# DeltaNet gate sums taken earlier, query sums and the second group's inverses later, six extra products at the last FFN

## The chip, the core and the metric

The kernel runs on one core of one Trainium2 chip, in one launch. The core has five engines that run side by side and each take their instructions strictly in the order in which the program gives them: TensorE (PE in the profile: matrix products and transposes into PSUM; PEld is its loading of weights), VectorE (DVE), ScalarE (ACT), GpSimd (POOL) and SyncE (SP, which here issues most DMAs). Semaphores tie them together: an instruction that waits holds up everything behind it on its own engine.

The metric is the device time of one execution in microseconds, lower is better. Before the change it is 1917.68 us, the median of three executions (1916.97 to 1921.42).

## What is computed

Two layers work on 256 context tokens and 256 latent tokens with 1024 channels. Each layer is a half-step SwiGLU FFN, a token mixer, and another half-step FFN; each of the three is preceded by an RMS norm with shift and scale, and added to the stream through a gate. The mixer of the first layer is a bidirectional gated DeltaNet in chunks of 64 tokens, that of the second is windowed attention. The output is the latent stream.

```python
def _swiglu(h, w1, w2):
    a, b = jnp.split(h @ w1, 2, axis=-1)
    return (jax.nn.silu(a) * b) @ w2

# DeltaNet, per head and chunk
gc = jnp.cumsum(_to_chunks(g, DN_CHUNK), axis=-1)
decay = jnp.exp(jnp.where(causal, gc[..., :, None] - gc[..., None, :], -jnp.inf))
kb = k * beta[..., None]
lower = jnp.where(strict, jnp.einsum('nhcid,nhcjd->nhcij', kb, k) * decay, 0.0)
uw = lax.linalg.triangular_solve(lower, rhs, left_side=True, lower=True, unit_diagonal=True)
qk = jnp.einsum('nhcid,nhcjd->nhcij', q, k) * decay
```

`g` and `beta` come from 32 columns of the input projection (the gates); `gc` are their running sums. `q` and `k` are projected, pass a short convolution over time and a SiLU, and are divided by their lengths, for which the sums of squares are needed. `triangular_solve` is the inverse of a 64 x 64 triangle for each chunk, head and direction.

## The kernel before

All activations lie with the channels on the 128 partitions and the 512 tokens (context, then latent) along the free dimension: 8 tiles of 128 x 512. The large products run in fp32r with each factor split in a high and a low part, three products in place of one (`mm3`). The weights stream in through SP's queue; ACT makes each high part, DVE or POOL the low one (`_split`).

**A planner writes the order.** The program is put out by Python generators ("tasks") under a small planner, `Sched`. It keeps a clock that each product advances by an assumed duration: in `mm`, 107 ns for an fp32r product of 256 columns and 213 for one of 512. It also keeps assumed times at which each tile will be ready. A task yields the time for which it wants to be left alone: `self.at(tile)` until the tile is expected, `self.spare(tile)` 2,500 ns longer. When the clock reaches a task's due time, its next step is put out, between two products of the main stream. The planner settles only the order on each engine's queue; on the chip the semaphores decide the time. While the main program waits in `Sched.until`, it puts out no products of its own, and the clock jumps from one due time to the next.

**The DeltaNet stage** (`deltanet`) projects 33 units through `units` and `halves_first`: the gates, then K, Z (an output gate), Q and V of heads 0 to 3, then K, V, Q and Z of heads 4 to 7. The first four units (gates, K heads 0 to 2) are done half by half, all context tokens first, 24 products of 256 columns for a unit's half. Each unit has a task `dn_unit`: ACT scales the product (the middle tap of the convolution), DVE adds four taps, ACT takes the SiLU; for K and V, PE transposes the result; for Q, ACT squares it; for Z, DVE applies a gain and the result is stored to DRAM (`ZD`).

Beside these run:
- `dn_gates`: softplus and sigmoid of the gates on ACT and DVE, the per-token values `gs` and `lb`; then five small fp32 products that sum `gs` over the chunk; then, out of the sums, `glb` and `kdl` on DVE, `eg` and `aS` on ACT, `neg` on DVE.
- `dn_kq(g)` for a group of four heads: `dn_ss` sums the squares of Q (four products with a matrix of ones), copies them to SBUF on ACT, transposes them and takes their logarithm (`lnq`, used by `dn_out` at the stage's end); then the key-query products (`dn_pairs`), multiplied on DVE with the decays. For group 1 it then stores Q and K to DRAM (`QD`, `KTD`).
- `dn_group(g)`: `dn_prep` (decay matrices), `dn_solve` (the inverses), then the four heads' recurrences `dn_chain` with `dn_expand`, which spreads the inverses and key-query blocks. For group 1 it waits for `kq_done[1]` and for group 0's chains, and then loads V, K, Q and the decayed K (`VD`, `KTD`, `QD`, `KD`) back from DRAM.
- `dn_solve` inverts 32 x 32 diagonal blocks in 31 steps on DVE, and then forms the off-diagonal blocks on PE, for each of two chunk pairs `qp`: 32 small products, a copy `w` on ACT, 32 products with `w`, and a write-back into `UB`.

**The last FFN** (`last_ffn`) works on latent tokens alone. Its norm ends in two products with a matrix of ones (`rstd`). The task `last_tokens` then transposes the eight activation tiles (16 transposes into four PSUM tiles), for the output is written with tokens on the partitions. Behind it `last_pairs` starts the FFN's first products as soon as the normed input `H` is there, tile by tile. `self.OH` are the attention's outputs, which lie in SBUF since the layer's middle.

Of the kernel before, what the change touches and what calls it, by code (L numbers as in the profile page):

```python
# [213 lines left out]
class Kernel:  # L214
# [706 lines left out]
    def last_tokens(self):  # L921

        nc = self.nc
        self.XT, self.gate = [], []

        while not self.rs_there:
            yield 100
        pss = []
        for tb in range(2):
            for fh in range(2):  # L930
                ps = self.mmt()
                for c in range(4):
                    self.tr(ps[:, 128 * c:128 * c + 128], self.X[4 * fh + c][:, 256 + 128 * tb:384 + 128 * tb])
                pss.append(ps)
        yield 8000
        for ps in pss:
            x = self.u()
            self.act(out=x, in_=ps, func=AF.Copy)
            self.XT.append(x)
            yield 1000  # L940
        pss = ps = None
        while (1, 8) not in self.ready:
            yield 1000
        gd = self.dp.tile([1024], F32, name="gd", tag="gd")
        nc.sync.dma_start(out=gd.rearrange("(k p) -> p k", p=128), in_=self.mod[1, 8][:, 1, :])
        for fh in range(2):
            g = self.u()
            nc.sync.dma_start(out=g, in_=gd[512 * fh:512 * fh + 512].partition_broadcast(128))
            self.gate.append(g)
            g = None  # L950
        yield 1000
# [250 lines left out]
    def dn_gates(self, ps):  # L1202

        nc = self.nc
        sb = self.u()
        for o, i in zip(self.pieces(sb, True), self.pieces(ps, False)):
            self.act(out=o[0:64], in_=i[0:64], func=AF.Copy)
        yield self.at(sb)
        p2 = self.cht()
        for q in range(4):  # L1210
            self.tr(p2[:, 64 * q:64 * q + 64], sb[0:64, 128 * q:128 * q + 128], 64)
        yield self.at(p2)
        t, y = self.u(), self.u()
        nc.vector.tensor_reduce(out=y[:, 0:128].rearrange("p (q c) -> p q c", q=4), axis=AX.X, op=ALU.add,
                                in_=p2[:, 0:256].rearrange("p (q j c) -> p q c j", q=4, j=2))
        x = t[:, 0:128].rearrange("p (q d k h) -> p q d k h", q=4, d=2, k=2)
        pv = y[:, 0:128].rearrange("p (q d k h) -> p q d k h", q=4, d=2, k=2)
        dtb = self.dtb.rearrange("p (d h) -> p d h", d=2).unsqueeze(1).broadcast_to([128, 4, 2, 8])
        nc.vector.tensor_tensor(out=x[:, :, :, 0, :], in0=pv[:, :, :, 0, :], in1=dtb, op=ALU.add)
        nc.vector.tensor_scalar(out=x[:, :, :, 1, :], in0=pv[:, :, :, 1, :], scalar1=-1.0, scalar2=None, op0=ALU.mult)  # L1220
        self.act(out=t[:, 128:256], in_=t[:, 0:128], func=AF.Abs)
        self.act(out=t[:, 256:384], in_=t[:, 128:256], func=AF.Exp, scale=-1.0)
        self.act(out=t[:, 384:512], in_=t[:, 256:384], func=AF.Ln, bias=1.0)
        nc.vector.scalar_tensor_tensor(out=t[:, 128:256], in0=t[:, 0:128], scalar=0.0, in1=t[:, 384:512],
                                       op0=ALU.max, op1=ALU.add)
        sp = t[:, 128:256].rearrange("p (q d k h) -> p q d k h", q=4, d=2, k=2)
        self.gs = self.const([128, 2, 4, 8], "gs")
        lb = self.const([128, 2, 4, 8], "lb")
        for e in range(2):
            for half in range(2):  # L1230
                d = e ^ half
                rw = slice(64 * half, 64 * half + 64)
                ea = self.ea[rw, 8 * d:8 * d + 8].unsqueeze(1).broadcast_to([64, 4, 8])
                nc.vector.scalar_tensor_tensor(out=self.gs[rw, e], in0=sp[rw, :, d, 0, :], scalar=-1.0, in1=ea,
                                               op0=ALU.mult, op1=ALU.mult)
                nc.vector.tensor_scalar(out=lb[rw, e], in0=sp[rw, :, d, 1, :], scalar1=-1.0, scalar2=None, op0=ALU.mult)
        yield self.spare(self.gs)
        p3 = self.cht()
        gf = self.gs.rearrange("p e q h -> p (e q h)")
        for e in range(2):  # L1240
            self.mm(p3[:, 32 * e:32 * e + 32], self.tri[e], gf[:, 32 * e:32 * e + 32])
        self.mm(p3[:, 64:128], self.bones, gf)
        for i in range(2):
            self.mm(p3[:, 128 + 64 * i:192 + 64 * i], self.hsel[i], gf)
        self.glb = self.const([128, 2, 4, 8], "glb")
        fl = lambda t: t.rearrange("p e q h -> p (e q h)")
        nc.vector.tensor_tensor(out=fl(self.glb), in0=p3[:, 0:64], in1=fl(lb), op=ALU.subtract)
        self.kdl = self.const([128, 2, 4, 8], "kdl")
        nc.vector.tensor_tensor(out=fl(self.kdl), in0=p3[:, 64:128], in1=fl(self.glb), op=ALU.subtract)
        self.eg = self.const([128, 2, 4, 8], "eg")  # L1250
        self.act(out=fl(self.eg), in_=p3[:, 0:64], func=AF.Exp)
        self.aS = self.const([128, 2, 2, 4, 8], "aS")
        self.act(out=self.aS.rearrange("p i e q h -> p (i e q h)"), in_=p3[:, 128:256], func=AF.Exp)
        self.neg = self.const([128, 2, 4, 8], "neg")
        nc.vector.tensor_scalar(out=self.neg, in0=self.eg, scalar1=-1.0, scalar2=None, op0=ALU.mult)
        self.kdw = self.const([128, 2, 4, 8], "kdw")
        self.mj = self.const([128, 2, 4, 8], "mj")
        self.lnk = self.const([128, 4, 8], "lnk")
        self.irho = self.const([128, 4, 8], "irho")
        self.lnq = self.const([128, 4, 8], "lnq")  # L1260
# [60 lines left out]
    def dn_ss(self, sq, g, dst):  # L1321

        ps = self.mmt()
        for i in range(4):
            self.mm(ps[32 * i:32 * i + 32, :], self.ones1, sq[4 * g + i], tp=(0, 32 * i), ns=230)
        sb = self.u()
        self.act(out=sb, in_=ps, func=AF.Copy)
        yield self.at(sb)
        ps = self.mmt()
        for q in range(4):  # L1330
            self.tr(ps[:, 128 * q:128 * q + 128], sb[:, 128 * q:128 * q + 128])
        self.act(out=dst[:, :, 4 * g:4 * g + 4], in_=ps.rearrange("p (q i r) -> p q i r", q=4, i=4)[:, :, :, 0],
                 func=AF.Ln, bias=self.eps)
        for i in range(4):
            del sq[4 * g + i]
# [93 lines left out]
    def dn_solve(self, g):  # L1429
# [53 lines left out]
        for qp in range(2):  # L1483
            combos = []
            for e in range(2):
                for half in range(2):
                    d = e ^ half
                    combos.append((d, 16 * e + 8 * qp, 64 * half + 32 * d, 64 * half + 32 * (1 - d), 32 * (1 - d)))
            ps = self.mmt()
            for i in range(8):  # L1490
                for d, x, ra, rb, cb in combos:
                    self.mm(ps[rb:rb + 32, 32 * i:32 * i + 32], UB[ra:ra + 32, x + i, cb:cb + 32],
                            v3(xt[d])[ra:ra + 32, x + i, :], tp=(ra, rb), ns=27)
            w = self.u()
            self.act(out=w[:, 0:256], in_=ps[:, 0:256], func=AF.Copy)
            wv = w[:, 0:256].rearrange("p (a i) -> p a i", i=32)
            yield self.at(w)
            ps = self.mmt()
            for i in range(8):
                for d, x, ra, rb, cb in combos:  # L1500
                    self.mm(ps[ra:ra + 32, 32 * i:32 * i + 32], wv[rb:rb + 32, i, :], UB[rb:rb + 32, x + i, cb:cb + 32],
                            tp=(rb, ra), ns=27)
            for n, (d, x, ra, rb, cb) in enumerate(combos):
                o, i = UB[ra:ra + 32, x:x + 8, cb:cb + 32], ps[ra:ra + 32, 0:256].rearrange("p (a i) -> p a i", i=32)
                if n % 2:
                    nc.vector.tensor_scalar(out=o, in0=i, scalar1=-1.0, scalar2=None, op0=ALU.mult)
                else:
                    self.act(out=o, in_=i, func=AF.Copy, scale=-1.0)
# [542 lines left out]
```

## Time and profile before

| | us |
|---|---|
| median of three executions | 1917.68 (1916.97 to 1921.42) |
| the profiled execution | 1922.17 |
| its span, first to last instruction | 1920.4 |
| DeltaNet stage, from the gates' products to the last chain | about 412 to 785 |
| attention stage | about 1595 to 1700 |
| last FFN | about 1721 to 1920 |

All later durations are read from the one profiled execution, in microseconds from the start of its span. In the timeline a row has its start, its duration (of several instructions together, where xN stands), engine, line, operation, what it writes and reads, and in brackets how long the engine had stood idle and what ended that. In rows of stretches stand from:to, length, then the busy time (and number of instructions) of PE, PEld, DVE, ACT and POOL, PE's granted clock, and the share of the DMA engines with GB/s. Nearly all instructions carry the line of a helper (L284 product, L289 transpose, L184 everything recorded for DVE, ACT, POOL and SP), so they are told apart by their tiles and shapes.

### The profile page before, as it was taken

The page shows a single profiled execution, that of the slowest core. Times are in us where ns is not written, and L with a number is a line of the kernel's source. Part 1 is how long each engine was busy: PE and PEld are TensorE (multiplying, and loading weights), DVE is VectorE, ACT ScalarE, POOL GpSimd, SP SyncE. Part 2 cuts the span into 40 slices and gives each one's busy share as a digit, 9 for nine tenths or more (in the row PEclk, how much of TensorE's full clock was granted, in tenths as well). Part 3 has the DMA queues.
Part 4 walks back from the last instruction along what each step waited for, and adds up shares of the span by engine and source line. Part 5 has one row for each costly group of instructions (what it writes and reads, how often), then busy time and mean ns, then how long its engine had stood idle before and what let it go on. Part 6 is the DMA issues. An engine that isn't in the chain of part 4 may idle for free.

```text
span 1920.4 us, 28976 instructions
## 1 busy us (share of the span) xinstructions
PE 1861.0 (97%) x10719; PEld 1525.2 (79%) x10719; DVE 1286.5 (67%) x2124; ACT 966.7 (50%) x2106; POOL 642.2 (33%) x594
## 2 busy tenths in 40 slices
PE   7999999998999999999999999999999999899998
PEld 5878888897777666798888888888888898688887
DVE  4887877755987965578787885745433345967565
ACT  4544534456466545465444444533332348867553
POOL 3343433353546535354343342321200047330000
PEclk9999999999999998999999999999999999999999
DMA  9655554413322252344555454455323325126561
GB/s 294 217 190 188 172 175 154 129 48 123 94 58 76 67 182 83 127 159 160 192 187 191 159 178 162 138 170 190 129 88 110 110 67 122 55 67 191 193 198 66
DMA packets 238708, 271.70 MB, mean 141 GB/s; under 512 B 12343, under 2 KB 189135, under 8 KB 238567
## 3 DMA queue, kind: packets, MB, share of 16 engines
q1 hardware_dynamic: 237703, 269.15, 43.4%
q8 instruction: 84, 1.38, 0.3%
q10 hardware_dynamic: 720, 0.59, 0.1%
q14 instruction: 57, 0.47, 0.1%
q0 software_dynamic: 144, 0.11, 0.0%
HBM read 259.32 MB, written 10.49 MB: 140 GB/s over the span
## 4 chain that ended last, share of the span: by engine, by line
PE 59%; DVE 9%; ACT 3%; issue 2%; POOL 1%; DMA 0%; DVEq 0%; POOLq 0%; ACTq 0%
PE mm L284 58%; DVE u L184 7%; ACT u L184 3%; DVE big L184 1%; PE mm L289 1%; POOL u L184 1%; DVE st L184 0%; DMA u<-XD 0%; ACT ub L184 0%; DVE ub L184 0%; ACT L184 0%; DVEq L184 0%; ACT sc L184 0%; POOLq L184 0%; ACTq L184 0%
## 5 line engine op out<-in xcount | busy, mean ns | idle before, releaser
L284 PE MATMUL mm<-u 128*128 128x512 f32 (+4 forms) x9480 | 1775.5, 353 | 21.5 <-POOL u L184 9.2
L284 PEld LDWEIGHTS mm<-u 128*128 128x128 f32 (+1 forms) x9480 | 1455.9, 185 | 325.1 <-issue 42.0
L184 POOL TENSOR_TENSOR u<-u 128x512 f32<-128x512 f32 (+4 forms) x386 | 425.6, 1108 | 903.9 <-ACT u L184 863.0
L184 ACT ACTIVATE u<-u 128x256 f32<-128x256 f32 (+8 forms) x361 | 170.9, 485 | 448.7 <-DVE u L184 435.4
L184 ACT ACTIVATE u<-mm 128x128 f32<-128x128 f32 (+5 forms) x382 | 152.0, 414 | 255.9 <-PE mm L284 174.2
L184 DVE TENSOR_TENSOR u<-raw,u 128x512 fp32r<-128x512 f32 (+2 forms) x270 | 220.0, 856 | 56.0 <-ACT u L184 55.9
L184 DVE SCALAR_TENSOR_TENSOR u<-u,cc 128x512 f32<-128x512 f32 x196 | 223.5, 1141 | 8.4 <-DMA u<-in_ada_w 5.2
L184 DVE TENSOR_TENSOR u<-ub,u 128x512 fp32r<-128x512 f32 x252 | 198.7, 831 | 30.7 <-ACT u L184 30.5
L184 ACT ACTIVATE u<-raw 128x512 fp32r<-128x512 f32 (+1 forms) x372 | 206.0, 607 | 8.2 <-PE mm L284 5.2
L184 ACT ACTIVATE u<-u,cc 128x512 f32<-128x512 f32 x224 | 151.8, 712 | 111.8 <-DMA u<-in_ada_w 102.7
L184 POOL TENSOR_TENSOR u<-raw,u 128x512 fp32r<-128x512 f32 x98 | 128.9, 1339 | 146.4 <-ACT u L184 116.5
L184 ACT ACTIVATE u<-ub 128x512 fp32r<-128x512 f32 (+1 forms) x282 | 156.4, 609 | 17.3 <-DVE u L184 8.2
L184 DVE TENSOR_TENSOR u<-u,mm 128x512 f32<-128x512 f32 x66 | 45.3, 686 | 164.1 <-PE mm L284 157.7
L184 DVE TENSOR_TENSOR u<-u 128x512 fp32r<-128x512 f32 (+5 forms) x158 | 98.3, 623 | 66.6 <-ACT u L184 63.3
L184 DVE SCALAR_TENSOR_TENSOR u<-mm,mod,u 128x256 f32<-128x256 f32 x168 | 74.6, 478 | 92.2 <-PE mm L284 91.8
L184 DVE SCALAR_TENSOR_TENSOR u<-u,mod 128x256 f32<-128x256 f32 (+1 forms) x140 | 88.5, 683 | 26.5 <-ACT u L184 26.2
L184 ACT ACTIVATE u<-u,mod 128x256 fp32r<-128x256 f32 (+1 forms) x124 | 56.1, 501 | 52.6 <-DVE u L184 51.8
L184 DVE SCALAR_TENSOR_TENSOR u<-mm,cw,u 128x510 f32<-128x510 f32 (+1 forms) x96 | 71.1, 742 | 11.7 <-ACT u L184 10.0
L289 PE MATMUL mm<-ident,u 128*128 128x128 f32 (+3 forms) x361 | 56.5, 292 | 23.0 <-ACT u L184 12.4
L289 PEld LDWEIGHTS mm<-ident,u 128*128 128x128 f32 (+3 forms) x361 | 43.9, 150 | 35.8 <-ACT u L184 16.4
L184 DVE TENSOR_TENSOR u<-mm,u 128x256 f32<-128x256 f32 (+2 forms) x102 | 41.6, 420 | 36.5 <-ACT u L184 16.2
L184 DVE SCALAR_TENSOR_TENSOR u<-u,aS,mm 128x128 f32<-128x128 f32 x96 | 31.0, 344 | 22.0 <-PE mm L284 21.5
(120 smaller groups left out, 601.5 us busy)
## 6 DMA issues: line engine op xcount, KB each, us to landing
u<-in_ada_w SPq DMA_DIRECT2D x256, 256.0 KB, 5.7
ub<-in_ffn_w SPq DMA_DIRECT2D x60, 1024.0 KB, 5.3
raw<-in_ffn_w SPq DMA_DIRECT2D x58, 1024.0 KB, 5.3
raw<-in_dn_w_in SPq DMA_DIRECT2D x16, 1024.0 KB, 5.7
ub<-in_ada_w SPq DMA_DIRECT2D x12, 512.0 KB, 7.3
ub<-in_ffn_w SPq DMA_DIRECT2D x6, 768.0 KB, 4.8
raw<-in_ffn_w SPq DMA_DIRECT2D x6, 768.0 KB, 5.1
raw<-in_dn_w_out SPq DMA_DIRECT2D x4, 1024.0 KB, 5.6
```

Source lines behind the costliest of these rows:

```text
L184: r = f(*a, **k)
L284: self.nc.tensor.matmul(out, lhsT, rhs, start=start, stop=stop, **kw)
L289: self.nc.tensor.transpose(out, in_, self.ident[:k, :k])
```

## The change

Four places change, and nothing that the output depends on.

- In `dn_gates` the sums of `gs` are due when `gs` is expected, and no longer 2,500 ns after that.
- In `dn_ss` (both groups) the transposes of the query sums are due 2,500 ns after their copy is expected, and no longer at once.
- In `dn_solve`, for the second group alone, each of the two steps that wait for `w` is due 2,000 ns later.
- In `last_tokens`, ahead of each of the first two groups of four transposes, three fp32r products of 256 columns are written into the PSUM tile that the transposes then overwrite. Their result is never read.

```diff
@@ last_tokens
                 ps = self.mmt()
+                if tb == 0:
+
+                    for i in range(3):
+                        self.mm(ps[:, 0:256], self.OH[0][7][:, 256:384], self.OH[0][6][:, 256:512])
                 for c in range(4):
                     self.tr(ps[:, 128 * c:128 * c + 128], self.X[4 * fh + c][:, 256 + 128 * tb:384 + 128 * tb])
@@ dn_gates
-        yield self.spare(self.gs)
+        yield self.at(self.gs)
         p3 = self.cht()
@@ dn_ss
         self.act(out=sb, in_=ps, func=AF.Copy)
-        yield self.at(sb)
+        yield self.spare(sb)
         ps = self.mmt()
@@ dn_solve
             wv = w[:, 0:256].rearrange("p (a i) -> p a i", i=32)
-            yield self.at(w)
+            yield self.at(w) + (2000.0 if g else 0.0)
             ps = self.mmt()
```

## The prediction

> **What bounds the kernel now.** I read the page's busy times, then stretches of the span, then the chain of waits, then the timeline at each edited place.
>
> ```profile
> PE 1861.0 (97%) x10719; PEld 1525.2 (79%) x10719; DVE 1286.5 (67%) x2124; ACT 966.7 (50%) x2106; POOL 642.2 (33%) x594
> ```
>
> ```profile
> 480.00:520.00 40.00, 38.08 (x167) 29.52 (x165) 38.34 (x54) 18.40 (x35) 27.63 (x25) 1.00 0.29 86
> 520.00:560.00 40.00, 35.89 (x275) 28.84 (x276) 38.64 (x67) 25.51 (x69) 12.32 (x11) 0.96 0.28 80
> ...
> 850.00:1200.00 350.00, 350.00 (x1665) 288.15 (x1664) 274.68 (x337) 164.66 (x295) 137.54 (x94) 1.00 0.52 175
> ```
>
> TensorE (PE) is the bound. After the DeltaNet stage it is busy in all of 350 us, so whatever that stage ends earlier, the whole kernel ends earlier. Inside the stage the bound changes: from 480 to 560 us VectorE (DVE, third pair of numbers) is busy in 38.3 and 38.6 of 40 us, so there a hole in PE's work costs little.
>
> The second thing to see is PE's granted clock (the number after the five engines). It is 1.00 or 0.50, and changes on a grid of 3.41 us. I laid stretches on that grid:
>
> ```profile
> 788.57:791.98 3.41, 1.77 (x6) 0.77 (x5) 3.31 (x8) 1.87 (x3) 0.00 (x0) 1.00 0.00 0
> 791.98:795.39 3.41, 3.41 (x9) 2.68 (x9) 0.55 (x2) 0.00 (x0) 0.00 (x0) 0.50 0.00 0
> 1641.90:1645.31 3.41, 2.30 (x13) 1.63 (x14) 3.34 (x10) 1.53 (x4) 0.91 (x2) 1.00 0.45 150
> 1645.31:1648.72 3.41, 3.41 (x35) 3.01 (x34) 3.21 (x12) 3.41 (x10) 0.82 (x2) 1.00 0.00 0
> 1648.73:1652.14 3.41, 1.92 (x12) 1.34 (x9) 3.31 (x8) 3.30 (x11) 3.04 (x3) 1.00 0.09 15
> 1652.14:1655.55 3.41, 2.45 (x30) 2.07 (x32) 3.25 (x12) 2.89 (x7) 0.00 (x0) 1.00 0.85 293
> 1723.82:1727.23 3.41, 1.81 (x12) 1.25 (x11) 2.83 (x7) 2.70 (x7) 1.02 (x1) 1.00 0.75 260
> 1727.23:1730.64 3.41, 3.00 (x9) 1.92 (x9) 3.13 (x7) 2.62 (x7) 1.56 (x2) 0.50 0.00 0
> 1730.65:1734.06 3.41, 3.41 (x11) 2.93 (x12) 1.37 (x3) 3.38 (x6) 0.73 (x1) 0.50 0.00 0
> ```
>
> A stretch in which PE was busy 1.77 or 1.81 us is followed by one at half clock; after 1.92 and 2.30 us the clock stays full. So the gate decides near 1.85 of 3.41 us. Where its grid falls is chance, and a hole may be cut by an edge of it in one execution and not in the next.
>
> **Gate sums (`spare` to `at`).** They come 2,500 planner ns earlier in the program's order. The planner's figures are used here for order alone: it charges 107 ns for a 256-column product, so the sums move ahead of 23 products of K head 2's projection; and ahead of one unit's convolution on DVE, since such a unit's latent half has 24 of these products.
>
> ```profile
> 427.29 8.05 PE L284 MATMUL mm<-u 128*128 128x256 f32 x64
> ...
> 433.40 1.29 DVE L184 SCALAR_TENSOR_TENSOR gs<-u,ea 64x32 f32<-64x32 f32 x1
> ...
> 435.18 0.53 PE L284 MATMUL mm<-gs,u 128*128 128x32 f32 x4
> ...
> 435.95 6.10 DVE L184 SCALAR_TENSOR_TENSOR u<-mm,cw,u 128x510 f32<-128x510 f32 x8
> 436.21 3.01 PE L284 MATMUL mm<-u 128*128 128x512 f32 x12
> ...
> 441.97 0.21 DVE L184 TENSOR_TENSOR glb<-mm,lb 128x64 f32<-128x64 f32 x1
> ...
> 442.54 0.22 ACT L184 ACTIVATE eg<-mm 128x64 f32<-128x64 f32 x1 [6.55 <-DVE kdl L184]
> ...
> 444.24 0.72 ACT L184 ACTIVATE u<-u 128x256 f32<-128x256 f32 x2
> ...
> 444.71 1.21 PE L289 MATMUL mm<-ident,u 128*128 128x128 f32 x4 [5.49 <-ACT u L184]
> ...
> 445.57 5.04 PE L284 MATMUL mm<-u 128*128 128x512 f32 x11
> ```
>
> Now: PE stands still for 5.49 us before K head 0's transposes. They wait for ScalarE's (ACT's) SiLU at 444.24; it is queued behind `eg`, which waits for `kdl`, which is queued on DVE behind eight convolution steps (two units), 435.95 to 442.05. The sums on PE had long been done, at 436.2.
>
> After: PE comes to the sums 23 x 0.126 (8.05/64) = 2.9 us earlier, at 432.3, and must wait there, because `gs` is ready no earlier than 433.40 + 1.29 = 434.7. So one wait becomes another: queued behind it are the 23 products, and for them waits only head 2's convolution, which DVE reaches after 442.05. The sums run as now, to 436.2; the 23 products end at 439.1. On DVE four convolution steps instead of eight stand ahead of `glb`: 435.95 + 3.05 = 439.0. From `glb` to the transposes it takes 444.71 - 441.97 = 2.74, so they can start at 441.7. By then PE has done about nine 512-column products at 0.25 (3.01/12); it did twelve by 444.71. Level: 441.7 + 3 x 0.25 = 442.5, a gain of 2.2. Then, today, eleven products take 5.04, 0.46 each, about twice the 0.25 and so half clock; at 0.25 that saves 11 x 0.21 = 2.3. Together 4.5. The new wait of 2.9 us and the short sums after it leave one stretch of the grid too idle in most executions, and 3.41 us at half clock lose 1.7 of products, of which some 0.3 would have been idle anyway; a third of the time an edge cuts the hole. I take **4.0**. Ends: 4.9 (cut by an edge, 0.4 of idle time filled) and -1.7 (`glb` stays behind both units, and the new half clock is paid). What is late next is head 1's SiLU, whose convolution ends about 1 us later than now; PE comes to it with products in hand. Behind this place PE is dense (38.08 of 40 us from 480 to 520), so the gain carries.
>
> The Trainium skill ("TensorE: Matmul & The Clock Gate", the table "Why this matters for your kernels") asks for no idle gap over about 3 us, and so would leave the new 2.9 us unpunished and make this term 4.5. The trace speaks for the smaller: the half clock at 791.98 follows a stretch with 1.77 us of work.
>
> **Query sums (`at` to `spare`), first group.**
>
> ```profile
> 517.71 1.89 PE L284 MATMUL mm<-u 128*128 128x512 f32 x7
> ...
> 521.35 0.72 ACT L184 ACTIVATE u<-u 128x256 f32<-128x256 f32 x2 [3.06 <-DVE u L184]
> ...
> 521.98 0.58 ACT L184 ACTIVATE u<-mm 128x512 f32<-128x512 f32 x1
> ...
> 522.61 1.12 PE L289 MATMUL mm<-ident,u 128*128 128x128 f32 x4 [3.02 <-ACT u L184]
> ```
>
> Four transposes wait 3.02 us for the copy at 521.98. Moved by 2,500 ns (twelve products at 213), they, the 32 key-query products and their DVE multiplications fall behind V head 0's transposes, which are due first. Those wait for the SiLU at 521.35, just ahead of the copy in ACT's queue: PE does three more products, then waits 1.9 instead of 3.0. It gets some 2.6 us ahead, but the stretch is DVE's (38.64 of 40), the multiplications leave it nothing fewer to do, and PE will wait at the next SiLU. I take **0.3**, ends 0 and 2.6. Nobody waits for the log of the sums before the stage's end.
>
> **Second group: its inverses (+2,000, twice) and its query sums (+2,500).**
>
> ```profile
> 685.58 0.34 SPq L184 DMA_DIRECT2D ZD<-u  x1
> ...
> 686.32 1.08 PE L284 MATMUL mm<-ub,u 32*32 32x32 f32 x64 [3.46 <-ACT u L184]
> ...
> 688.18 1.73 PE L284 MATMUL mm<-u,ones 128*32 128x512 f32 x8
> ...
> 694.94 1.80 SPq L184 DMA_DIRECT2D u<-KD  x4
> ...
> 697.38 0.52 DVE L184 COPY u<-ub 64x256 f32<-64x256 f32 x2
> ...
> 698.01 1.36 PE L284 MATMUL mm<-u 128*128 128x128 f32 x9 [0.42 <-PE mm L284]
> ```
>
> ```profile
> DMA to landing us min/median/max: 3.8/5.7/6.7
> ```
>
> The code waits here for group 1's chains and puts out no other projection, so a delay is not time on the chip but an exchange: the sums' eight products (1.73) go ahead of the inverses' second products into the hole of 3.46, and the key-query products ahead of the second pair's. The inverses and the expansion copy at 697.38 may be done some 2 us earlier. But group 1's chain also needs its reloads: SP's queue holds ZD, eight stores and then the loads of VD, KD, KTD and QD, none moved past another, and the first KD load lands at 694.94 + 3.8 = 698.7, 0.7 after the chain's start. So the loads cap the gain: **0.5**, ends +0.7 and -6.5 (all delays real).
>
> **Six products at the last FFN.**
>
> ```profile
> 1702.86 18.46 PE L284 MATMUL mm<-u 128*128 128x256 f32 x150 [0.37 <-ACT u L184]
> ...
> 1722.88 1.91 PE L289 MATMUL mm<-ident,u 128*128 128x128 f32 x16
> ...
> 1725.64 0.62 PE L284 MATMUL mm<-u 128*128 128x512 f32 x2 [0.85 <-DVE u L184]
> ...
> 1730.80 0.73 POOL L184 TENSOR_TENSOR u<-u 128x256 fp32r<-128x256 f32 x1 [0.47 <-ACT u L184]
> ```
>
> They cost 6 x 0.123 (18.46/150) = 0.74 of PE, and the transposes behind them end at 1724.8 + 0.7 = 1725.5. The 0.85 of waiting for the normed input hides this; without that cover they would cost the 0.74. They can gain the clock: 1.81 busy in the stretch from 1723.82 becomes about 2.5, above the gate. The half clock from 1727.23 (6.8 us, two stretches) loses less than 3.4, because until 1731.5 (1730.80 + 0.73) PE waits for input; from there to 1734.06 it loses half of 2.5, **1.3**. But the next stretch is full of such waits and may trip the gate instead. Half of 1.3: **0.6**, ends -0.7 and 1.3.
>
> ```profile
> 1641.90:1645.31 3.41, 1.22 (x5) 0.80 (x6) 1.00 0.45 150
> ...
> 1723.82:1727.23 3.41, 0.84 (x3) 0.52 (x4) 1.00 0.75 260
> ```
>
> These are the same stretches with products alone, transposes left out. The same page (Part 4, PE-mode transpose) says that transposes don't count as busy for the gate. By it 0.84 + 0.74 = 1.6 stays under the gate, and this term is 0. The trace contradicts: 1.22 of products, with transposes beside them to 2.30, kept the clock. By that rule the sum would be 4.8 instead of 5.4.
>
> **Sum:** 4.0 + 0.3 + 0.5 + 0.6 = 5.4 us. The profiled execution took 1922.17 (span 1920.4 and 1.8 around it), which would become 1916.8. It lies 4.5 above the median of the three runs, within their spread; the half clocks by chance are my reason to count from the median: 1917.68 - 5.4 = **1912.3**.
>
> **Rivals.**
> - *All of it comes* (chance 0.25): no half clock at the new wait, PE's lead of 2.6 is used, the last FFN keeps its clock: 4.5 + 2.6 + 0.7 + 1.3 = 9.1, 1908.6. For it: PE is 97% busy over all. Against: DVE's 38.6 of 40.
> - *The wait only moves* (0.20): `glb` isn't freed from both units, or the new hole costs two stretches of half clock; gate 0 to 1, the rest 0 to 1: 1916.7. For it: the sums' input is at 434.7 in either order.
> - *Group 1 starts late* (0.10), slower: the key-query products reach PE later, the loads are issued behind them, and the chain starts late by the delays that come true, up to 6.5; against the gate's 4.0 that gives 1920.2, and 1924.2 if the gate gives nothing. It decides from where the first KD load, now issued at 694.94, lies 0.7 later, since from there the chain waits for it.
>
> **How the numbers follow.** The forecast has 0.45 (1909.5 to 1915). This kernel's measurement tells 0.3%, 5.75 us, from no change: faster means below 1911.9. That takes half of the forecast's 0.45 and nearly all of the 0.25: 0.46. Slower (above 1923.4) is part of the last rival: 0.07. The rest, 0.47, is within. Range 1905 to 1919.5: from the full gain with a luckier clock, to the late start with half the gate's gain.
>
> **What would show it.** Gate: a PE wait of 2 to 3 us ahead of the sums near 432, `glb` after four convolution steps, transposes at about 441.7 instead of 444.7, and prep's first product 4 us earlier. Query sums: V's transposes ahead of them, and DVE still without holes. Second group: the sums' eight products straight behind the inverses' first products, KD's issue unmoved against ZD's. Last FFN: clock 1.00 up to some 1731. I am wrong if the stage's end, seen where the dense FFN starts, hasn't moved by 3 to 6 us, or if it moved for another reason.

## The result: slower, 1939.7 us

| | before | after |
|---|---|---|
| median, us | 1918.51 (1916.97 to 1921.42, 4 runs) | 1939.72 (1939.65 to 1941.6, 4 runs) |
| ratio to before | | 1.0102, 95% interval 1.0088 to 1.0116 |
| span of the profiled execution, us | 1920.4 | 1937.9 |

The forecast was 1912.3 with a range to 1919.5; the change is about 20 us slower. The mechanisms that it gave for the gate sums and for the last FFN are there in the traces; what it gave the least thought to, the query sums, cost more than everything else brought.

Busy times, from the page of after:

```profile
PE 1873.4 (97%) x10725; PEld 1532.8 (79%) x10725; DVE 1283.3 (66%) x2124; ACT 965.6 (50%) x2106; POOL 642.6 (33%) x594
```

No engine has more to do, apart from six products. PE's share is 97% as before; its busy time is 12.4 us longer, at a mean granted clock of 0.983 in place of 0.989. The page alone doesn't say where the time went. For that I followed the same instructions through both traces:

| instruction | before | after | difference |
|---|---|---|---|
| group 0's preparation, `lnk` (ACT) | 462.36 | 458.01 | -4.4 |
| last products of group 0's inverses begin (PE) | 558.76 | 555.32 | -3.4 |
| group 1's preparation, `lnk` (ACT) | 579.11 | 575.73 | -3.4 |
| group 1's inverses begin: two large transposes (DVE) | 602.52 | 603.55 | +1.0 |
| group 1's inverses end: transposes back (DVE) | 675.36 | 689.86 | +14.5 |
| group 1's recurrence begins: its first products of 64 rows (PE) | 699.53 | 712.25 | +12.7 |
| norm after DeltaNet (ACT) | 817.23 | 833.84 | +16.6 |
| norm of the last FFN (ACT) | 1723.08 | 1741.14 | +18.1 |
| end of the span | 1920.4 | 1937.9 | +17.5 |

Up to 579 the change is ahead. Some 18 us are lost between 579 and 690, before the delayed steps of the second group's inverses are reached (these come after 697). Its delayed query sums do fall into that time: in after their transposes begin at 677.79, before at 691.52. Another 4 us go between the start of group 1's recurrence and the norm; from there to the end of the span the distance stays between 16.6 and 18.1, as is to be expected of a dense PE.

**Where they go.** The stretch from the start to the end of group 1's inverses, in the columns of the rows of stretches (length, PE, PEld, DVE, ACT, POOL, clock, DMA): before,

```profile
602.50:675.40 72.90, 71.98 (x467) 51.90 (x463) 67.23 (x147) 45.88 (x146) 41.89 (x59) 1.00 0.23 72
```

and after:

```profile
603.50:689.90 86.40, 77.47 (x530) 55.53 (x530) 66.94 (x154) 48.08 (x147) 40.55 (x61) 0.93 0.26 86
```

Read the third pair of numbers: VectorE does the same amount of work, 67.23 and 66.94 us, but needs 86.4 us for it in place of 72.9. It stands idle for 19.5 us; it was 5.7. What it waited for in these stretches, before:

```profile
DVE u L184 <- ACT u L184: 2.2, 2, 1.3
DVE u L184 <- PE mm L284: 1.7, 3, 1.1
```

and after (us in total, times, longest):

```profile
DVE u L184 <- PE mm L284: 10.1, 14, 2.4
DVE u L184 <- ACT u L184: 7.5, 5, 2.8
```

The inverses themselves need no other engine while their 31 steps run. These are waits of other instructions, queued on VectorE between the steps. VectorE's timeline at the start of the inverses, before:

```profile
595.26 1.11 DVE L184 SCALAR_TENSOR_TENSOR u<-mm,neg,u 128x128 f32<-128x128 f32 x4
596.29 2.30 DVE L184 SCALAR_TENSOR_TENSOR u<-mm,cw,u 128x510 f32<-128x510 f32 x3
598.62 1.49 DVE L184 COPY big<-ub 32x1024 f32<-32x1024 f32 x2
600.15 0.75 DVE L184 SCALAR_TENSOR_TENSOR u<-mm,cw,u 128x508 f32<-128x508 f32 x1
600.81 1.79 DVE L184 SCALAR_TENSOR_TENSOR u<-u,aS,mm 128x128 f32<-128x128 f32 x6
602.52 4.16 DVE L184 STREAM_TRANSPOSE big<-big 128x1024 f32<-128x1024 f32 x2
```

and after:

```profile
594.75 2.30 DVE L184 SCALAR_TENSOR_TENSOR u<-mm,cw,u 128x510 f32<-128x510 f32 x3
596.97 1.11 DVE L184 SCALAR_TENSOR_TENSOR u<-mm,neg,u 128x128 f32<-128x128 f32 x4
598.11 2.39 DVE L184 COPY big<-ub 32x1024 f32<-32x1024 f32 x2
600.54 3.10 DVE L184 SCALAR_TENSOR_TENSOR u<-mm,cw,u 128x510 f32<-128x510 f32 x4
603.55 3.80 DVE L184 STREAM_TRANSPOSE big<-big 128x1024 f32<-128x1024 f32 x2
607.26 1.07 DVE L184 SCALAR_TENSOR_TENSOR u<-u,aS,mm 128x128 f32<-128x128 f32 x4
```

The rows with `neg` and `aS` belong to group 0's recurrence (`dn_chain`), those with `cw` to the projections' convolutions. Before, the recurrence's `neg` step stands ahead of the convolution, and its state updates (`aS`) ahead of the transposes. After, a unit's convolution has gone ahead of both, and the updates stand behind the transposes, at 607.26 in place of 600.81. So the projections run ahead of the recurrence. That can be counted in the traces: how many 512-column products of the projections PE had begun when a given instruction of VectorE began. The program puts out 624 of them; then it waits in `Sched.until` for group 1's chains and holds back the last three Z units (72 products) until they exist.

| | before | after |
|---|---|---|
| first state update of group 0's recurrence | 424 | 429 |
| its 9th (second step) | 450 | 474 |
| its 48th, the last | 588 | 624 |
| end of group 1's inverses | 607 | 624 |

Five products at first, then 24, a whole unit with its four convolution steps, and at the end all 624. The same in times: the first update comes at 583.60 before and 580.24 after, the ninth at 600.81 and 607.26, the last at 667.71 and 683.28. So the recurrence, 3.4 us ahead at first, is 6.4 behind by the ninth update and 15.6 by the last. The projections run the other way: their 622nd product begins at 681.3 before and at 673.7 after.

With them used up, little is left to run beside the rest of the recurrence and of the inverses, which are queued among each other. Of the 62 instructions of the inverses' steps, the first 54 take 69.8 us in after (67.5 before), and from there to the transposes back it takes 16.5 us (5.3 before). PE's stretch without a projection, from the 624th product to the first of the held-back ones, grows from 12.3 us (681.8 to 694.1) to 24.2 (682.0 to 706.2). VectorE at the end of the inverses, before, does one step behind another:

```profile
670.03 0.48 DVE L184 TENSOR_TENSOR u<-big 128x112 f32<-128x112 f32 x1
670.54 0.28 DVE L184 TENSOR_TENSOR big<-big,u 128x112 f32<-128x112 f32 x1
670.85 0.25 DVE L184 TENSOR_TENSOR u<-big 128x87 f32<-128x87 f32 x1
671.14 0.25 DVE L184 TENSOR_TENSOR big<-big,u 128x87 f32<-128x87 f32 x1
671.30 0.34 DVE L184 SCALAR_TENSOR_TENSOR u<-mm,neg,u 128x128 f32<-128x128 f32 x1
```

and after:

```profile
679.52 1.29 DVE L184 TENSOR_TENSOR u<-mm,u 128x512 f32<-128x512 f32 x2 [2.39 <-PE mm L284]
680.73 0.59 DVE L184 SCALAR_TENSOR_TENSOR u<-u,aS,mm 128x128 f32<-128x128 f32 x2
681.24 0.24 DVE L184 TENSOR_TENSOR u<-big 128x87 f32<-128x87 f32 x1
...
683.53 0.24 DVE L184 TENSOR_TENSOR big<-big,u 128x87 f32<-128x87 f32 x1
686.31 0.49 DVE L184 TENSOR_SCALAR u<-u,ogain 128x512 f32<-128x512 f32 x1 [2.53 <-ACT u L184]
686.71 0.21 DVE L184 TENSOR_TENSOR u<-big 128x60 f32<-128x60 f32 x1
```

An inverse step of 0.24 us (`big`) comes once in 2 to 3 us; ahead of it stand group 1's key-query multiplications, waiting 2.39 us for PE, and Z's gain, waiting 2.53 us for ACT. And PE in turn. Before, it runs projections beside the end of the inverses; after, the last two begin at 681.7 and 682.0.

```profile
671.73 10.45 PE L284 MATMUL mm<-u 128*128 128x512 f32 x60
```

```profile
678.33 4.69 PE L284 MATMUL mm<-u 128*64 128x64 f32 x84
688.62 0.77 PE L284 MATMUL mm<-u 128*128 128x128 f32 x2 [5.60 <-DVE u L184]
```

In after it waits 5.60 us for VectorE's `neg` result, which was queued behind that gain.

### The profile page after: what moved, and what is told of

The parts are those of the page before. It is cut to its first block, busy times and chain, and to the rows that moved or that the text cites. A ratio compares the mean times of both kernels' runs of the same rounds, so it can differ in the third digit from the quotient of the medians.

```text
span 1937.9 us, 28993 instructions
## 1 busy us (share of the span) xinstructions
PE 1873.4 (97%) x10725; PEld 1532.8 (79%) x10725; DVE 1283.3 (66%) x2124; ACT 965.6 (50%) x2106; POOL 642.6 (33%) x594
## 4 chain that ended last, share of the span: by engine, by line
PE 82%; DVE 11%; ACT 4%; issue 2%; POOL 1%; DMA 0%; POOLq 0%; DVEq 0%; ACTq 0%
PE mm L284 80%; DVE u L184 9%; ACT u L184 3%; PE mm L289 2%; DVE big L184 1%; POOL u L184 1%; DVE st L184 0%; DMA u<-in_ada_b 0%; ACT L184 0%; DVE ub L184 0%; ACT ub L184 0%; DVE gs L184 0%; DVE lb L184 0%; POOLq L2051 0%; DVEq L184 0%
## 5 line engine op out<-in xcount | busy, mean ns | idle before, releaser
L284 PE MATMUL mm<-u 128*128 128x512 f32 (+4 forms) x9486 | 1785.2, 354 | 33.6 <-DVE u L184 12.7
L284 PEld LDWEIGHTS mm<-u 128*128 128x128 f32 (+2 forms) x9486 | 1461.4, 185 | 342.2 <-issue 51.1
L184 POOL TENSOR_TENSOR u<-u 128x512 f32<-128x512 f32 (+5 forms) x386 | 425.1, 1107 | 918.9 <-ACT u L184 873.7
L184 ACT ACTIVATE u<-u 128x512 fp32r<-128x512 f32 (+8 forms) x361 | 170.9, 485 | 455.4 <-DVE u L184 439.2
L289 PE MATMUL mm<-ident,u 128*128 128x128 f32 (+3 forms) x361 | 58.9, 298 | 18.1 <-DVE u L184 6.6
```

The costliest lines, as they stand in the source:

```text
L184: r = f(*a, **k)
L284: self.nc.tensor.matmul(out, lhsT, rhs, start=start, stop=stop, **kw)
L289: self.nc.tensor.transpose(out, in_, self.ident[:k, :k])
```

## The experiments

The first four kernels take the edits one by one.

**The gate sums alone.**

```diff
-        yield self.spare(self.gs)
+        yield self.at(self.gs)
```

> The gate sums alone (one line of the four edits). Theory A (the loss comes from the query sums, whose delay changes the order of group 0's chain steps, the convolutions and group 1's inverses): this kernel keeps the 4.35 us that the start of DeltaNet's preparation gained in the trace of the full change, and ends 3 to 5 us earlier than before, 1913.5 to 1915.5. Rival B (an earlier preparation is itself what collides with the projections' convolutions): the loss is here, 10 to 20 us slower, 1928 to 1938. Rival C (the loss is half clock that falls where chance puts it): within 3 us of before, and the trace shows other places of half clock than either kernel.

Measured: ratio 0.9972 (0.9961 to 0.9982), 5.4 us faster (3.5 to 7.5). In the trace `lnk` comes at 455.26, 7.1 us earlier than in before's, and the distance is still 7.3 at the norm after DeltaNet (809.87). An earlier preparation harms nothing: B falls.

**The query sums alone**, in both groups.

```diff
-        yield self.at(sb)
+        yield self.spare(sb)
```

> The query sums' delay alone, in both groups. Theory A: all of the loss and none of the gains. The full change is 21.2 us slower; without the gate's 4.4 and the last FFN's 0.6 this one is about 26 slower, 1944.7, and in any case over 15 slower; solve(1)'s first products come 15 us or more later than before's 682.1. Rival B (gate): within 3 us of before, 1916 to 1921. Rival C (chance of the half clock): between 0 and 10 slower, with the start of solve(1)'s products within 5 us of before's.

Measured: 1.0124 (1.0111 to 1.0137), 1944.62 us, 23.8 slower. The last products of group 1's inverses begin 19.3 later (701.45), at the same counts of products as in after (429, 474, 624). The whole loss is here, and B and C fall. The second group's delay, by itself, changes no engine's order; whether it has a part in the loss beside the first group's, with its transposes inside the stretch that got longer, was not measured.

**The second group's inverses alone.**

```diff
-            yield self.at(w)
+            yield self.at(w) + (2000.0 if g else 0.0)
```

> The second group's inverses 2,000 planner ns later, alone. Theory A: within 2 us of before, 1916.5 to 1920.5, since the full change is late before this step is reached. Rival D (the delays of the second group come true on the chip): up to 4 us slower, 1922.5, with the recurrence of group 1 starting up to 4 later than 699.53.

Measured: 0.9994 (0.9985 to 1.0003), 1.2 us faster with an interval that holds zero. D falls.

**The six products alone.**

```diff
+                if tb == 0:
+                    for i in range(3):
+                        self.mm(ps[:, 0:256], self.OH[0][7][:, 256:384], self.OH[0][6][:, 256:512])
```

> The six products alone. By the prediction 0.6 us faster, 1917.9 (between 1.3 faster and 0.7 slower). If they keep the clock full at 1727 to 1734, the trace shows clock 1.00 there and the time from the last FFN's norm to the end is 0.6 to 1.3 shorter; if transposes don't count as work for the gate, the clock is 0.50 there as before and the end 0 to 0.7 later.

Measured: 0.9996 (0.9987 to 1.0006), 0.8 faster, zero within the interval. The clock is 1.00 from 797 to 1920 in its trace, and from the last FFN's norm to the end it takes 196.8 us (before 197.3).

**The change without the query sums.**

> The full change without the query sums' delay: gate sums, second group's inverses and the six products. Theory A: the three gains stand alone and add up: the gate's 5.4 (ratio 0.9972) and about 1 each for the two others, 1911.5 to 1914.5, a ratio of 0.994 to 0.997 to before. Rival F (the edits spoil each other, so that the sum of the singles doesn't hold): 1917 or more.

Measured: 0.9951 (0.9938 to 0.9964), 1911.85 us. The three other edits keep their gains, some 9 us together, and F falls. This beats both kernels.

The next question was whether late query sums cost, or the order that they leave behind.

**Query sums 500 planner ns later still**, first group only.

```diff
-        yield self.at(sb)
+        yield self.at(sb) + (3000.0 if g == 0 else 0.0)
```

> The first group's query sums delayed by 3,000 planner ns in place of 2,500 (second group unchanged). They and the 32 key-query products come still later, behind V head 0's transposes and two products further than in the full change, but the planner's clock is back in step by the time of the inverses' products, so that the order of everything behind them is before's. Theory A (the loss is the new deal of the order behind, not the query sums' own lateness): within 2 us of before, ratio 0.999 to 1.001, solve(1)'s first products within 1.5 us of 682.1. Rival G (late query sums and key-query products cost by themselves): at least as slow as with 2,500, over 20 us slower.

Measured: 0.9993 (0.9984 to 1.0002). More delay, and no loss at all. The counts are 424, 450, 588 and 607, before's to the last product. G falls.

**The full change with that one number.**

```diff
-        yield self.spare(sb)
+        yield self.spare(sb) + (500.0 if g == 0 else 0.0)
```

> The full change with one number changed: the first group's query sums 3,000 planner ns later in place of 2,500; all four edits are in. Theory A: the order behind is before's again, so the 21.2 us go and the other edits' gains show: 1909.5 to 1913, a ratio of 0.993 to 0.996. If the full change loses by late query sums as such, it stays above 1935.

Measured: 0.9963 (0.9952 to 0.9975), 1912.92 us: 500 planner ns turn a loss of 20 us into a gain of 7, with the second group's delay left in. Its stretch of group 1's inverses:

```profile
596.70:669.60 72.90, 72.00 (x467) 51.90 (x463) 67.25 (x147) 45.88 (x146) 41.95 (x59) 1.00 0.23 72
```

The same 72.9 us and the same count of instructions on PE, DVE and ACT as before.

**Another deal without touching the query sums.** The last step of group 0's inverses, for which the recurrence waits, is due later, by 1,600 or 2,200 planner ns.

```diff
-        yield self.at(*xt)
+        yield max(0.0, self.at(*xt) + (2200.0 if g == 0 else 0.0))
```

> Before, with the query sums untouched: the last step of group 0's inverses (from the two transposes to the write-back) is due 2,200 planner ns later. That shifts what is behind them (group 0's recurrence, group 1's preparation) against the projections by four products, in another deal than the full change's five. Theory J (the deal of before is tuned and any shift of the recurrence against the projections costs): 8 to 25 us slower. Rival K (only the deal that the full change hit is bad): within 4 us of before.

> As the run before, with 1,600 ns: a shift by one product. Theory J: 4 to 20 us slower. Rival K: within 4 us of before.

Measured: 1.008 (1.0065 to 1.0095) and 1.003 (1.0021 to 1.0039), 15.4 and 5.8 us slower. J holds twice and K falls: it isn't the query sums alone, since two other orders in which the projections get ahead of the recurrence cost as well. An order in which the recurrence gets ahead of the projections was not run.

| kernel | products before 1st, 9th and last update | inverses, us | DVE idle in them | against before, us |
|---|---|---|---|---|
| before | 424, 450, 588 | 72.8 | 5.7 | |
| query_3000 | 424, 450, 588 | 72.1 | 5.3 | -1.3 |
| full_3000 | 424, 450, 588 | 72.8 | 5.6 | -7.1 |
| tail_1600 | 425, 454, 603 | 78.7 | 9.4 | +5.8 |
| tail_2200 | 428, 474, 600 | 83.4 | 17.2 | +15.4 |
| query_only | 429, 474, 624 | 86.0 | 18.6 | +23.8 |

Where the counts are before's, there is no loss, and where the second is higher, there is one. That the count sets the loss is argued from this, not shown: with the same 474, tail_2200 loses 15.4 and query_only 23.8.

The last four try to find the one wait that does it.

**State updates behind the transposes, nothing else.** Before, with the transposes earlier: four of the updates come to stand behind them, and no other order changes.

```diff
-        yield self.at(dg)
+        yield max(0.0, self.at(dg) + (-2000.0 if g else 0.0))
```

> Before, with one change: the two large transposes at the start of group 1's inverses are due 2,000 planner ns earlier. The only difference in any engine's order is that four of the state updates of group 0's recurrence (two heads) stand behind these two transposes on VectorE instead of ahead of them. The transposes took 2.0 and 2.1 us. Theory A' (the loss begins where the recurrence's state updates are queued behind these transposes, and the recurrence is what the stage's end waits for): the two heads are some 4 us late and the stage's end with them, 2 to 5 us slower than before, ratio 1.001 to 1.0025. Rival H (these chains have slack there, the loss arises elsewhere): within 1 us of before, or faster, since the inverses start 1 us earlier.

Measured: 1.0008 (0.9998 to 1.0017), 1.5 slower, zero within the interval. In its trace the last products of the inverses begin 2.1 later and the norm after DeltaNet comes 3.0 later. If the place has a price, then by the interval one of at most some 3 us for four of the six updates that got behind in after.

**The updates put ahead again**, with the query sums' delay.

```diff
-        yield self.at(dg)
+        yield max(0.0, self.at(dg) + (7000.0 if g else 0.0))
```

> The query sums' delay in both groups, with the two large transposes of group 1's inverses 7,000 planner ns later, so that all eight state updates of group 0's recurrence stand ahead of them on VectorE again; the convolutions that had come ahead of the recurrence stay where the delay put them, and the inverses start later. Theory A' (that one place holds most of the loss): half or more of the 24 us comes back, 1925 to 1934. Rival I (the loss is the whole new deal, convolutions ahead of both the recurrence and the inverses, and no single place): less than 8 us comes back, 1937 to 1946.

Measured: 1.0163 (1.0149 to 1.0176), 1952.4 us. Not only did nothing come back, it is 8 us slower than the delay alone: the recurrence's 9th update is 2.2 us earlier, but the inverses begin 5.0 later and last as long (85.6), and the recurrence's last update ends 4.3 later as well (691.5 and 687.2). A' falls as the main cause. The 2.2 us at the start of the recurrence were lost again within it.

**PE's holes filled.**

```diff
+            for _ in range(8 if h == 0 and s == 7 else 0):
+                self.mm(ps[:, 128:256], self.ident, self.ident, ns=0.0)
             self.mm(ps[:, 128:256], U, r)
...
             ps = self.mmt()
+            for _ in range(2 if g else 0):
+                self.mm(ps[:, 0:128], self.ident, self.ident, ns=0.0)
             for i in range(8):
```

> The query sums' delay in both groups, with 16 products of no use (128 columns, fp32) on PE where it waited in that kernel: eight ahead of the last step of group 0's first recurrence (into the hole of 5.60 us), two ahead of each of the four sets of 32 small products of group 1's inverses. No other engine's order changes. The clock was 0.50 from 688.27 to 712.16 there. Theory L (the half clock takes a good part of the loss): the clock is full in most of that stretch, group 1's recurrence starts 3 to 8 us earlier than 716.36, and the whole is 3 to 8 us faster than with the delay alone, 1937 to 1942. Rival M (the waits are those of VectorE and ScalarE, PE's clock decides nothing there): as slow as with the delay alone, 1943 to 1947, or up to 6 slower by the products themselves.

Measured: 1.0136 (1.0117 to 1.0155), 1946.06 us, as slow as the delay alone; by the two intervals the filling can have gained 2 us at most. The same stretch in the kernel with the delay alone,

```profile
688.27:712.16 23.89, 15.17 (x299) 10.94 (x300) 11.28 (x19) 11.64 (x37) 6.74 (x11) 0.50 0.88 318
```

and with the holes filled:

```profile
688.94:712.84 23.90, 16.28 (x328) 13.46 (x328) 11.13 (x17) 10.85 (x35) 6.74 (x11) 0.71 0.89 314
```

The granted clock rose from 0.50 to 0.71, so about 10 of the 24 us went from half to full clock, and no gain of L's 3 to 8 us came of it. L expected a full clock in most of the stretch; what the half clock that is left costs isn't shown.

**Key-query multiplications of group 1 behind the inverses.**

```diff
+        if g:
+            yield 9000.0
         for qp in range(2):
             ps = self.mmt()
             self.dn_pairs(ps, self.kT, self.qT, g, qp)
```

> The query sums' delay in both groups, with group 1's key-query products and their four multiplications on VectorE 9,000 planner ns later: behind the last steps of group 1's inverses again, as they stand before. The inverses otherwise keep the delayed kernel's place. Theory N (the idle time of VectorE inside the inverses comes from instructions queued ahead of their steps that wait for PE and ScalarE; at 679 to 686 these are the multiplications): the 2.4 and 0.3 us of waiting and some 2.5 of work leave the inverses' stretch, which ends 3 to 6 us earlier than 693.4, and the whole is 2 to 6 faster than with the delay alone, 1938.5 to 1942.5. Rival O (group 1's recurrence waits for the key-query products anyway): the inverses end earlier, the whole doesn't, 1943 to 1947.

Measured: 1.0117 (1.01 to 1.0134), 22.5 slower than before where the delay alone is 23.8. The inverses last 80.5 us in place of 86.0, as N had it, and group 0's last update ends 3.2 earlier (684.0 and 687.2), but group 1's recurrence begins only 0.9 earlier (715.5 and 716.4): the key-query products, which it needs too, begin at 691.2 in place of 681.9. The interval doesn't separate it from the delay alone; the trace is O's.

**Inverse steps put out further ahead.**

```diff
-            yield max(0.0, self.s.free["vector"] - self.s.clock - self.solve_lag)
+            yield max(0.0, self.s.free["vector"] - self.s.clock - (4000.0 if g else self.solve_lag))
```

> The query sums' delay in both groups, with the steps of group 1's inverses put out up to 4,000 planner ns ahead of VectorE's assumed time in place of 800, so that fewer recurrence steps with waits stand between them. Theory N: VectorE's idle time inside the inverses (18.7 us with the delay alone, 5.7 before) falls to 6 to 12, the inverses take 73 to 80 us in place of 86.0, and the whole is 6 to 13 faster than with the delay alone, 1931.5 to 1938.5. Rival P (the recurrence itself is what ends last; held back it gives the time back): the inverses get shorter and group 1's recurrence starts no earlier than 714, 1941 or more.

Measured: 1.017 (1.0154 to 1.0185), 1952.07 us. The inverses last 74.8 us, nearly before's 72.8, and the kernel is 8 us slower than with the delay alone. VectorE's timeline behind them:

```profile
708.79 0.35 DVE L184 SCALAR_TENSOR_TENSOR u<-u,aS,mm 128x128 f32<-128x128 f32 x1 [1.05 <-PE mm L284]
...
712.95 0.35 DVE L184 SCALAR_TENSOR_TENSOR u<-u,aS,mm 128x128 f32<-128x128 f32 x1 [1.06 <-PE mm L284]
713.62 0.35 DVE L184 SCALAR_TENSOR_TENSOR u<-u,aS,mm 128x128 f32<-128x128 f32 x1 [0.33 <-PE mm L284]
```

Now group 0's recurrence is what is late. Its last update ends at 714.0 (with the delay alone at 687.2, before at 668.1), and group 1's recurrence begins at 729.9. P holds.

Taken together: group 1's recurrence needs the end of group 0's recurrence, that of group 1's inverses, and group 1's key-query products. Before, the first two end 7 us apart, at 668.1 and 675.4, with projections beside them to the end. With the delay, three runs each brought something forward, and something else came later; none made up for the loss. So no single one of the waits tried is the cause. That it is the projections run ahead which leave these parts to wait for each other fits all the traces, but no run put the projections alone back.

## Why the prediction was wrong

- **Query sums, first group: the step that failed.** It read: "I take 0.3, ends 0 and 2.6", and argued from the timeline at 517 to 523, where the step is put out. There it was right: the query sums and the key-query products stand behind V head 0's transposes, and with the delay alone the last products of group 0's inverses begin only 0.4 us later than before (559.17 and 558.76). What it left out is that each later due time in the planner hangs on its clock and on its assumed busy time of VectorE, so that one moved step moves all later tasks against the products of the main stream. Here they moved by five products, and 60 to 170 us later that became a unit, then all of the projections ahead of the hold. The term was put at 0.3 us faster; with both groups' delays it measured 23.8 us slower. The size of the delay says nothing about that: 3,000 for the first group cost nothing, 2,500 all of it.
- **"The multiplications leave it nothing fewer to do."** True, and no argument. VectorE's work is the same to 0.3 us in both orders of the inverses' stretch; its idle time isn't. An engine at 92% (67.23 of 72.90) can get slower without a single instruction more.
- **The rivals** all lay at the edited places. None was a new order between 580 and 690, and so the range ended at 1919.5. The slower one, "group 1 starts late", didn't happen as a mechanism: it was to decide from the first load of KD, and that was issued at 694.41 in after (694.94 before), 17.8 ahead of a recurrence that began 12.7 later.
- **Gate sums.** The mechanism was right in each link. After's timeline:

```profile
434.81 0.41 PE L284 MATMUL mm<-gs,u 128*128 128x32 f32 x2 [0.48 <-DVE gs L184]
436.46 0.41 PE L284 MATMUL mm<-gs,u 128*128 128x32 f32 x2 [1.24 <-DVE gs L184]
...
443.40 0.85 PE L289 MATMUL mm<-ident,u 128*128 128x128 f32 x4 [1.21 <-ACT u L184]
```

```profile
437.65 3.10 DVE L184 SCALAR_TENSOR_TENSOR u<-mm,cw,u 128x510 f32<-128x510 f32 x4
440.67 0.21 DVE L184 TENSOR_TENSOR glb<-mm,lb 128x64 f32<-128x64 f32 x1
```

  PE waits for `gs`, `glb` stands behind four convolution steps and no longer eight, and the wait ahead of the transposes falls from 5.49 to 1.21 us. The half clock that began between 443 and 446 is in all twelve profiles without this edit and in none of the four with it. Measured was 5.4 (3.5 to 7.5), which holds the 4.0; the term may have been too small. I had charged a new wait of 2.9 us and a half clock for it; the wait was 0.48 + 1.24 = 1.7, and the clock behind it is full in after. The 4.4 us at `lnk` in the table are less than the edit's gain in that trace, because `gs` itself came 1.75 later there (its last product with `ea` begins at 435.15, before at 433.40).
- **Second group.** 0.5 was predicted, 1.2 measured for the inverses' delay alone, with zero in its interval. Not refuted. In full_3000 the order is as described: PE runs the sums' products behind the inverses' first products, and the chain then waits a little for the loads, as the prediction had it:

```profile
694.18 2.06 PE L284 MATMUL mm<-u 64*128 64x128 f32 x14 [0.39 <-DMA u<-KD]
```

- **Six products.** 0.6 was predicted, 0.8 measured with zero in its interval; the trace decides. The last FFN's first stretches of the grid in after, all instructions and then products alone:

```profile
1739.80:1743.21 3.41, 2.82 (x24) 2.76 (x24) 1.03 (x4) 1.91 (x5) 0.08 (x1) 1.00 0.62 199
1743.21:1746.62 3.41, 2.20 (x11) 1.28 (x10) 3.23 (x7) 2.53 (x6) 1.86 (x2) 1.00 0.32 109
1746.62:1750.03 3.41, 2.32 (x10) 1.28 (x10) 1.79 (x4) 3.34 (x6) 1.46 (x2) 1.00 0.00 0
```

```profile
1739.80:1743.21 3.41, 1.67 (x9) 1.21 (x8) 1.00 0.62 199
```

  The clock stays full after a stretch with 2.82 us of work, of which 1.67 are products and the rest transposes; from the norm to the end it takes 196.7 us in place of 197.3, the 0.6 of the forecast. All four profiles with the six products have full clock there (196.1 to 196.8 us), and three of the twelve without (query_3000, transposes_early and query_inverse_ahead, 196.7 to 196.8); the nine with half clock take 197.3 to 198.5. By the Trainium skill ("TensorE: Matmul & The Clock Gate", Part 4, PE-mode transpose) a transpose "doesn't count as PE-busy the same way". If it didn't count at all, 1.67, less than the 1.77 of products that was followed by half clock before, would have brought it here; the trace says that transposes count. Plainer still is query_3000, here all instructions and then products alone:

```profile
1719.59:1723.00 3.41, 1.86 (x14) 1.31 (x12) 2.55 (x6) 2.68 (x8) 1.00 (x1) 1.00 0.83 283
1723.00:1726.42 3.42, 2.19 (x8) 1.20 (x8) 3.17 (x7) 2.65 (x7) 1.57 (x3) 1.00 0.00 0
```

```profile
1719.59:1723.00 3.41, 0.62 (x2) 0.30 (x2) 1.00 0.83 283
```

  With 0.62 us of products and 1.86 in all the clock stays full.
- **The gate's limit.** "Near 1.85 of 3.41 us" is the middle of a band, and no sharp limit. In after, 2.07 us of work were followed by half clock:

```profile
767.00:770.41 3.41, 2.07 (x18) 1.49 (x18) 2.78 (x10) 1.82 (x6) 0.06 (x1) 1.00 0.99 325
770.41:773.82 3.41, 2.70 (x16) 1.62 (x15) 2.32 (x8) 1.25 (x6) 1.64 (x4) 0.50 0.99 341
```

  In the sixteen traces, from 300 us on, all 53 stretches at full clock with under 1.57 us of work were followed by half clock and none with over 2.22; between the two both came.
- **The sum.** Without the query sums, the terms come to 4.0 + 0.5 + 0.6 = 5.1; measured were 9.4 (6.9 to 11.9), more than forecast. The three single runs add up to 7.4. That the DeltaNet stage's gain carries to the end was right as well: gate_only is 7.1 ahead at `lnk` and 6.6 at the end of the span. Three slips in the working change little: between 439.1 and 441.7 fit ten products of 0.25 and not nine; 1.4 us lost two times in three take 0.9 off the 4.5, which leaves 3.6 and not 4.0; and 1922.17 lies above the highest of the three runs (1921.42).

What stays open: the first group's delay was not run without the second's at 2,500 ns, nor was one of the held-back Z units put out earlier, which might fill PE's stretch without projections; and the last 4 us of the loss in after, between the start of group 1's recurrence and the norm after DeltaNet, were not taken apart.

## What to carry to other kernels

Where a planner deals out the order from its own clock, an edit's price isn't at its place alone: list each engine's new order against the old one all the way down, and count how much work of the main stream stands ahead of each dependent sequence; if that count moves, the edit has to be priced there. An engine that is not the busiest in the stretch is at risk too (here VectorE, at 92%), because the same amount of work in another order can leave it idle. And before a delay is dropped or kept for its time, run it with a slightly different number: if the time jumps, it is the deal that was measured and not the edit.

## What the runs showed of the hardware

Half clock isn't always a loss. With the query sums' delay alone PE was granted 0.50 for 23.9 us on end and was busy for 15.17 of them; with 16 further products the same stretch had 0.71, and the time was the same within the intervals (1.0124 and 1.0136 to before). In that stretch PE waited for other engines, and a higher clock bought no time that the runs can tell.
